# A two-layer decoder trunk on one core: opening with matmuls on constants, sums of squares on VectorE, two loads in halves, small tiles padded

## The chip, the cores and the metric

The kernel runs on one core of one Trainium2 chip. The time is device microseconds (us) from the start to the end of one execution, the median of several runs. The five engines that matter are TensorE (PE in the profile, its weight loads PEld), VectorE (DVE), ScalarE (ACT), GpSimd (POOL) and the queue SP, which here issues most of the DMAs.

## What is computed

The reference is a trunk of two residual layers over 256 tokens of width 2048, all in float32. The pieces that matter here are the norm and the input projection of the first layer:

```python
h = x
hn = rmsnorm(h, norm_w[0])            # x * rsqrt(mean(x*x) + eps) * w
proj = hn @ w_in                      # 2048 -> 12320 columns
z_a, xbc, dt_raw, z_b, u, v = split(proj)
xbc = silu(causal_depthwise_conv(xbc, conv_w, conv_b))   # x, B and C of the scan
dt = softplus(dt_raw + dt_bias)
```

Then come a chunked state-space scan over 32 heads in 8 groups, a gated spatial mixing of 16 groups, an output projection, a second layer of differential attention with 16 heads, its output projection, and a last RMSNorm.

## The kernel before

**Layout.** Activations are kept transposed, channels on the partitions: `xw` holds the normed input as 16 blocks (k = 0 to 15) of 128 channels by 256 tokens. Float32 precision is kept by splitting each operand in a high half, rounded to the matmul's reduced float32 (`fp32r`), and a low half, which is the rest. For activations `put_split` (L202) does this: ScalarE writes the high half (L204), VectorE the low one (L205). For weights `split` (L115) does it: ScalarE writes `wh` (L118), VectorE `wl` (L119), on 1024 elements a partition at a time.

**Projections.** Weights come in tiles of 128 x 2048 (1 MB) in the order in which they are used; `fetch` (L122) loads one with one DMA on SP, `halves` (L127) splits it in two halves. `t_half` (L132) takes one half: a run of eight matmuls of 512 columns, `wh` against high and low activations together (L136), and a run of eight of 256 columns, `wl` against the high activations (L140). A block of 128 output channels is two halves, thus 16 matmuls of either kind. `tok_proj` (L159) computes 512 channels for all tokens with three products a step (L170 to L172). There are three buffers each for the raw weights, `wh` and `wl`.

**Order.** The tile framework orders the instructions of every engine ahead of time: each engine takes, of what its estimate says is ready, the instruction that stands first in the program text. The chip then runs each engine's instructions strictly in that order. `issue_after` sets what it encloses behind a given instruction on the engine of that instruction.

**The opening (L209 to L262).** SP loads x in pieces (the first in two halves), the small weight `wdt` of the dt projection, and the first two weight tiles (`raw_first`, those of B and C) in halves, all interleaved: x first half, `wdt`, x second half, then by turns half a weight tile and the next four blocks of x. `wd` is `wdt` split into high and low columns (L240, L241). The loop at L243 splits each block of x into `xw` and multiplies it for dt (L245). Then B and C are multiplied by halves (`t_half`, L136 and L140). The norm's factor isn't in `xw`; it is applied behind the projections. It is made at L253 to L262: ScalarE squares x behind the last split of the opening (L256), POOL adds the sixteen blocks up (L257 to L261), and `token_rstd` (L181) sums over the partitions with a matmul against `ones` (L187), takes the power -1/2 on POOL (L191) and spreads the result over the partitions with a matmul against `ident` (L194), to `rb` (L199).

**What follows.** Blocks x0_0 and x0_1 are the next two projections (`conv_block`, L326), then B1, C1, x1_0, x1_1 and the gate z. The dt stage (L265 to L317) makes dt from `pdt` with `rt0`: an exponential, then a series in some 17 small POOL operations (L290 to L302), two transposes on TensorE (L305), a cumulative sum (L309), and its way to all partitions through DRAM.

**Constants.** At L90 to L104: `col` (per-channel constants) by ScalarE's DMA queue, then on POOL `ident`, `ones`, `mhalf`, `maskT` and two small loads. `ms` (L177, L184) is a tile of two numbers a partition, two buffers of it, in a pool that also holds larger temporary tiles; the pools allocated behind that one hold `xw`, `ya` and everything after.

```python
def t_half(ps, hv, x, half, first, last):
    wh, wl = hv
    for i in range(8):                                       # L134 to L137
        k = half * 8 + i
        pe.matmul(ps, lhsT=wh[:, i, :], rhs=x[:, k, :, :].rearrange("p a b -> p (a b)"), start=first and k == 0, stop=False)
    for i in range(8):                                       # L138 to L141
        k = half * 8 + i
        pe.matmul(ps[:, 256:512], lhsT=wl[:, i, :], rhs=x[:, k, 0, :], start=False, stop=last and k == 15)
```

Of the kernel before, what the change touches and what calls it, by code (L numbers as in the profile page):

```python
# [9 lines left out]
F32 = mybir.dt.float32  # L10
F32R = mybir.dt.float32r
AF = mybir.ActivationFunctionType
ALU = mybir.AluOpType
# [4 lines left out]
P = 128  # L18
# [54 lines left out]
def hybrid_trunk(ctx: ExitStack, tc: tile.TileContext, xT, cols, dskip, dtp, lnw, lnb, sgub, wsT,  # L73
                 wdt, w0, wo0, w1, wo1, outT):
    nc = tc.nc
    v, act, pe, pool = nc.vector, nc.scalar, nc.tensor, nc.gpsimd

    const = ctx.enter_context(tc.tile_pool(name="const", bufs=1))
    wp = ctx.enter_context(tc.tile_pool(name="wp", bufs=3))
    ev = ctx.enter_context(tc.tile_pool(name="ev", bufs=2))  # L80
# [5 lines left out]
    def aux(name):  # L86
        return aux_p.tile([P, 512], F32, tag="aux", name=name)


    col = const.tile([P, N_COLS], F32, name="col")  # L90
    act.dma_start(col, cols)
    ident = const.tile([P, P], F32, name="ident")
    make_identity(nc, ident)
    ones = const.tile([P, P], F32, name="ones")
    pool.memset(ones, 1.0)
    mhalf = const.tile([P, 2], F32, name="mhalf")
    pool.memset(mhalf, -0.5)
    maskT = const.tile([P, P], F32, name="maskT")
# [10 lines left out]
    def c1(i):  # L109
        return col[:, i:i + 1]  # L110


    last_split = [None, None]

    def split(raw, shape, nm):  # L115
        wh = wp.tile([P] + shape, F32R, tag="wh", name=f"wh_{nm}")
        wl = wp.tile([P] + shape, F32R, tag="wl", name=f"wl_{nm}")
        last_split[0] = act.activation(wh, raw, AF.Copy).ins  # L118
        last_split[1] = v.tensor_tensor(wl, raw, wh.bitcast(F32), op=ALU.subtract).ins  # L119
        return wh, wl  # L120

    def fetch(src, nm):  # L122
        raw = wp.tile([P, 2048], F32, tag="raw", name=f"raw_{nm}")
        nc.sync.dma_start(raw, src)
        return raw

    def halves(src, inner, nm):  # L127
        raw = fetch(src, nm).rearrange("p (a b) -> p a b", b=inner)
        n = 2048 // inner // 2
        return [split(raw[:, h * n:(h + 1) * n, :], [n, inner], f"{nm}_{h}") for h in range(2)]  # L130

# [11 lines left out]
    def t_accum(ps, src, x, first, last, nm):  # L143

        hv = halves(src, P, nm)
        for half in range(2):
            t_half(ps, hv[half], x, half, first, last)

    def acc(nm):
        return acc_p.tile([P, 512], F32, tag="acc", name=f"acc_{nm}")  # L150
# [8 lines left out]
    def tok_proj(srcs, x, nm):  # L159
        ps = [acc(f"{nm}_{i}") for i in range(2)]  # L160
        for kq in range(4):
            hv = halves(srcs[kq], 512, f"{nm}_{kq}")
            for kk in range(4):
                k = kq * 4 + kk
                wh, wl = hv[kk // 2]
                wh, wl = wh[:, kk % 2, :], wl[:, kk % 2, :]
                for tb in range(2):
                    xh = x[:, k, 0, tb * P:(tb + 1) * P]
                    xl = x[:, k, 1, tb * P:(tb + 1) * P]
                    pe.matmul(ps[tb], lhsT=xh, rhs=wh, start=k == 0, stop=False)  # L170
                    pe.matmul(ps[tb], lhsT=xh, rhs=wl, start=False, stop=False)  # L171
                    pe.matmul(ps[tb], lhsT=xl, rhs=wh, start=False, stop=k == 15)  # L172
        return ps

    def pow_mhalf(dst, ssum, n, scale, nm):

        ms = ev.tile([P, 2], F32, tag="ms", name=f"ms_{nm}")  # L177
        v.tensor_scalar(ms[:, :n], ssum, scale, EPS, op0=ALU.mult, op1=ALU.add)
        pool.tensor_tensor(dst, ms[:, :n], mhalf[:, :n], op=ALU.pow)

    def token_rstd(sqs, nm, copy=True):  # L181

        pcs = [aux(f"pc{tb}_{nm}") for tb in range(2)]
        ms = ev.tile([P, 2], F32, tag="ms", name=f"ms_{nm}")  # L184
        for tb in range(2):
            for i, sq in enumerate(sqs):
                pe.matmul(pcs[tb][:, 0:1], lhsT=sq[:, tb * P:(tb + 1) * P], rhs=ones[:, 0:1],  # L187
                          start=i == 0, stop=i == len(sqs) - 1)
            v.tensor_scalar(ms[:, tb:tb + 1], pcs[tb][:, 0:1], 1.0 / D, EPS, op0=ALU.mult, op1=ALU.add)
        rt = const.tile([P, 2], F32, tag="rt", name=f"rt_{nm}", bufs=2)  # L190
        pool.tensor_tensor(rt, ms, mhalf, op=ALU.pow)  # L191
        pb = aux(f"pb_{nm}")
        for tb in range(2):
            pe.matmul(pb[:, tb * P:(tb + 1) * P], lhsT=rt[:, tb:tb + 1].broadcast_to([P, P]),  # L194
                      rhs=ident, start=True, stop=True)
        if not copy:
            return rt, pb[:, 0:S]
        rb = const.tile([P, S], F32, tag="rb", name=f"rb_{nm}", bufs=1)
        act.activation(rb, pb[:, 0:S], AF.Copy)  # L199
        return rt, rb  # L200

    def put_split(dst, src, scale):  # L202

        act.activation(dst[:, 0, :], src, AF.Copy, scale=scale)  # L204
        v.scalar_tensor_tensor(dst[:, 1, :], src, scale, dst[:, 0, :].bitcast(F32),  # L205
                               op0=ALU.mult, op1=ALU.subtract)


    with ExitStack() as l0:  # L209
        s1 = l0.enter_context(tc.tile_pool(name="ssd1", bufs=1))  # L210

        sqs = s1.tile([P, S], F32, name="sqs")
# [8 lines left out]
        def split_first(i, half):  # L221
            raw = first[i][0][:, half * 1024:(half + 1) * 1024].rearrange("p (a b) -> p a b", b=P)
            first[i][1][half] = split(raw, [8, P], f"first{i}_{half}")

        with tc.tile_pool(name="start", bufs=4) as st:
            wdt_raw = st.tile([P, KB, 32], F32, name="wdt_raw", bufs=1)
# [10 lines left out]
                first_half(i % 2, i // 2)  # L237
            wd = st.tile([P, KB, P], F32R, name="wd", bufs=1)
            pool.memset(wd[:, :, 64:128].bitcast(F32), 0.0)
            act.activation(wd[:, :, 0:32], wdt_raw, AF.Copy)  # L240
            v.tensor_tensor(wd[:, :, 32:64], wdt_raw, wd[:, :, 0:32].bitcast(F32), op=ALU.subtract)  # L241
            pdt = acc("dt")
            for k in range(KB):  # L243
                put_split(xw[:, k], xr[k // 4][:, k % 4, :], c1(C_NW0 + k))
                pe.matmul(pdt, lhsT=wd[:, k, :], rhs=xw[:, k].rearrange("p a b -> p (a b)"),  # L245
                          start=k == 0, stop=k == KB - 1)
                if k % 4 == 3:
                    split_first(k // 4 % 2, k // 8)
# [4 lines left out]
            sq = st.tile([P, 4, 4, S], F32, name="sq", bufs=1)  # L253
            with tc.issue_after(last_split[0]):
                for i in range(4):
                    act.activation(sq[:, i], xr[i], AF.Square)  # L256
            pool.tensor_tensor(sq[:, 0], sq[:, 0], sq[:, 1], op=ALU.add)  # L257
            pool.tensor_tensor(sq[:, 2], sq[:, 2], sq[:, 3], op=ALU.add)
            pool.tensor_tensor(sq[:, 0], sq[:, 0], sq[:, 2], op=ALU.add)
            pool.tensor_tensor(sq[:, 0, 0:2], sq[:, 0, 0:2], sq[:, 0, 2:4], op=ALU.add)  # L260
            pool.tensor_tensor(sqs, sq[:, 0, 0, :], sq[:, 0, 1, :], op=ALU.add)  # L261
            rt0, rb0 = token_rstd([sqs], "n0")  # L262


# [152 lines left out]
        def ssd_finish(g, y, sz):  # L417
            n = f"g{g}"
            v.tensor_tensor(y, y, sz[:, :, (g % 2) * S:(g % 2 + 1) * S], op=ALU.mult)
            ss = sp.tile([P, 2], F32, tag="ss", name=f"ss_{n}")  # L420
            for c in range(2):
                junk = sp.tile([P, S], F32, tag="junk", name=f"junk_{n}_{c}")
                act.activation(junk, y[:, c, :], AF.Square, accum_out=ss[:, c:c + 1])
            rg = sp.tile([P, 2], F32, tag="rg", name=f"rg_{n}")
            pow_mhalf(rg, ss, 2, 1.0 / S, n)
            for c in range(2):
                act.activation(y[:, c, :], y[:, c, :], AF.Copy, scale=rg[:, c:c + 1])
            ps4 = aux(f"ps4_{n}")
            for b in range(2):
                for c in range(2):  # L430
                    pe.transpose(ps4[:, b * S + c * P:b * S + (c + 1) * P], y[:, c, b * P:(b + 1) * P], ident)
            for b in range(2):
                put_split(ya[:, 2 * g + b], ps4[:, b * S:(b + 1) * S], c1(C_SNW + 2 * g + b))
# [13 lines left out]
    with ExitStack() as l0b:  # L447
# [13 lines left out]
        for tb in range(2):  # L461
            junk = gp_.tile([P, D], F32, tag="junk", name=f"vjunk{tb}", bufs=1)
            act.activation(junk, vt[:, tb, :], AF.Square, bias=nmu[:, tb:tb + 1], accum_out=vq[:, tb:tb + 1])
        vr = g1.tile([P, 2], F32, name="vr")
        pow_mhalf(vr, vq, 2, 1.0 / D, "ln")
        ws_t = sb_t = None
        for j in range(16):
            n = f"j{j}"
# [33 lines left out]
            for c in range(2):  # L502
                pe.matmul(pm[:, c * P:(c + 1) * P], lhsT=vt[:, c, j * P:(j + 1) * P], rhs=ws_t[:, j % 4, :],
                          start=True, stop=True)
# [46 lines left out]
    act.dma_start(res, xT)  # L551
    sqp = out_proj(wo0, "o0", lambda n: put_split(xw[:, n], res[:, n, :], c1(C_NW1 + n)))
    rt1, rb1 = token_rstd(sqp, "n1")


# [127 lines left out]
    n = 0  # L683
# [70 lines left out]
```

## Time and profile before

| | |
|---|---|
| median of 3 runs | 1724.22 us (1722.86 to 1724.52) |
| the profiled execution: its time | 1724.63 us |
| the profiled execution: its span | 1722.9 us |
| TensorE matmuls: busy, share, count | 1702.2 us, 99%, 9232 |
| TensorE weight loads: busy, share | 1460.7 us, 85% |
| VectorE: busy, share, instructions | 1126.6 us, 65%, 1704 |
| ScalarE: busy, share, instructions | 990.1 us, 57%, 1521 |
| POOL: busy, share, instructions | 106.0 us, 6%, 159 |
| moved by DMA | 318.68 MB, mean 185 GB/s |

The profile is one execution recorded by the chip. The span goes from its first instruction to its last; the execution's own time is 1.7 us longer. Busy shares are averages over the whole span. Matmuls are pipelined, so that the durations of neighbours overlap; the distance between starts tells their rate. In the rows, "a<-b" names what is written and what is read, "[0.70 <-ACT wh_first]" is idle time of that engine just before the instruction and what ended it, "x8" merges eight instructions.

### The profile page before, as it was taken

The page shows a single profiled execution, that of the slowest core. Times are in us where ns is not written, and L with a number is a line of the kernel's source. Part 1 is how long each engine was busy: PE and PEld are TensorE (multiplying, and loading weights), DVE is VectorE, ACT ScalarE, POOL GpSimd, SP SyncE. Part 2 cuts the span into 40 slices and gives each one's busy share as a digit, 9 for nine tenths or more (in the row PEclk, how much of TensorE's full clock was granted, in tenths as well). Part 3 has the DMA queues.
Part 4 walks back from the last instruction along what each step waited for, and adds up shares of the span by engine and source line. Part 5 has one row for each costly group of instructions (what it writes and reads, how often), then busy time and mean ns, then how long its engine had stood idle before and what let it go on. Part 6 is the DMA issues. An engine that isn't in the chain of part 4 may idle for free.

```text
span 1722.9 us, 23833 instructions
## 1 busy us (share of the span) xinstructions
PE 1702.2 (99%) x9232; PEld 1460.7 (85%) x9232; DVE 1126.6 (65%) x1704; ACT 990.1 (57%) x1521; POOL 106.0 (6%) x159
## 2 busy tenths in 40 slices
PE   7999999999999999999999999999999999999997
PEld 6888888888888888888888888888888888888886
DVE  6897869545777665556566666757576666655554
ACT  6776776546777744445455555555554555555443
POOL 3200000100000011110000000000000000001110
PEclk9999999999999999999999999999999999999998
DMA  7555444655655565555455455455545555445552
GB/s 254 207 175 195 172 159 171 218 198 191 216 205 173 194 236 184 193 194 172 172 188 177 171 173 191 173 173 173 184 169 184 174 180 184 171 172 196 195 191 104
DMA packets 46290, 318.68 MB, mean 185 GB/s; under 512 B 5280, under 2 KB 5584, under 8 KB 9440
## 3 DMA queue, kind: packets, MB, share of 16 engines
q1 hardware_dynamic: 44400, 310.30, 51.3%
q0 software_dynamic: 1344, 4.24, 0.9%
q10 hardware_dynamic: 432, 2.61, 0.4%
q8 instruction: 72, 1.18, 0.3%
q14 instruction: 42, 0.34, 0.1%
HBM read 315.00 MB, written 2.13 MB: 184 GB/s over the span
## 4 chain that ended last, share of the span: by engine, by line
PE 95%; DVE 1%; ACT 1%; issue 1%; POOL 1%; DMA 0%; SPq 0%; DVEq 0%; POOLq 0%; ACTq 0%
PE acc_o L136 13%; PE acc_q L136 7%; PE acc_k L136 7%; PE acc_o L140 7%; PE acc_v L170 5%; PE acc_v L172 5%; PE acc_v L171 5%; PE acc_q L140 3%; PE acc_g L172 3%; PE acc_k L140 3%; PE acc_g L170 3%; PE acc_g L171 3%; PE acc_u L136 3%; PE acc_zb L136 3%; PE acc_x L136 3%; PE acc_u L140 2%
## 5 line engine op out<-in xcount | busy, mean ns | idle before, releaser
L118 ACT ACTIVATE wh_v<-raw_v 128x1024 fp32r<-128x1024 f32 x96 | 101.8, 1060 | 109.1 <-PE acc_v L172 88.7
L119 DVE TENSOR_TENSOR wl_v<-raw_v,wh_v 128x1024 fp32r<-128x1024 f32 x96 | 117.6, 1225 | 68.3 <-ACT wh_v L118 67.4
L171 PE MATMUL acc_v<-wl_v,xw 128*128 128x512 f32 x384 | 152.2, 396 | 0.0
L172 PE MATMUL acc_v<-wh_v,xw 128*128 128x512 f32 x384 | 151.6, 395 | 0.0
L170 PE MATMUL acc_v<-wh_v,xw 128*128 128x512 f32 x384 | 142.8, 397 | 0.0
L136 PE MATMUL acc_q<-xw,wh_q 128*128 128x512 f32 x512 | 131.8, 393 | 0.0
L119 DVE TENSOR_TENSOR wl_g<-raw_g,wh_g 128x1024 fp32r<-128x1024 f32 x64 | 78.4, 1226 | 80.6 <-ACT wh_g L118 80.6
L136 PE MATMUL acc_k<-xw,wh_k 128*128 128x512 f32 x512 | 130.8, 395 | 0.0
L118 ACT ACTIVATE wh_g<-raw_g 128x1024 fp32r<-128x1024 f32 x64 | 67.9, 1060 | 80.5 <-PE acc_g L172 53.5
L119 DVE TENSOR_TENSOR wl_q<-raw_q,wh_q 128x1024 fp32r<-128x1024 f32 x64 | 77.8, 1225 | 52.0 <-ACT wh_q L118 46.5
L118 ACT ACTIVATE wh_k<-raw_k 128x1024 fp32r<-128x1024 f32 x64 | 67.8, 1059 | 70.2 <-PE acc_q L136 30.2
L118 ACT ACTIVATE wh_q<-raw_q 128x1024 fp32r<-128x1024 f32 x64 | 67.8, 1059 | 68.3 <-PE acc_g L172 23.9
L136 PEld LDWEIGHTS acc_k<-xw,wh_k 128*128 128x128 f32 x512 | 91.6, 188 | 16.2
L136 PEld LDWEIGHTS acc_q<-xw,wh_q 128*128 128x128 f32 x512 | 90.5, 188 | 15.6
L172 PE MATMUL acc_g<-wh_g,xw 128*128 128x512 f32 x256 | 101.5, 397 | 0.0
L171 PE MATMUL acc_g<-wl_g,xw 128*128 128x512 f32 x256 | 101.0, 394 | 0.0
L119 DVE TENSOR_TENSOR wl_k<-raw_k,wh_k 128x1024 fp32r<-128x1024 f32 x64 | 78.3, 1224 | 26.8 <-ACT wh_k L118 26.7
L170 PE MATMUL acc_g<-wh_g,xw 128*128 128x512 f32 x256 | 92.2, 396 | 0.0
L170 PEld LDWEIGHTS acc_v<-wh_v,xw 128*128 128x128 f32 x384 | 72.0, 187 | 16.5
L172 PEld LDWEIGHTS acc_v<-wh_v,xw 128*128 128x128 f32 x384 | 72.0, 188 | 16.3
L171 PEld LDWEIGHTS acc_v<-wl_v,xw 128*128 128x128 f32 x384 | 72.0, 188 | 16.0
L140 PE MATMUL acc_q<-xw,wl_q 128*128 128x256 f32 x512 | 73.8, 281 | 0.0
(500 smaller groups left out, 4012.6 us busy)
## 6 DMA issues: line engine op xcount, KB each, us to landing
raw_v<-in_w_dram SPq DMA_DIRECT2D x48, 1024.0 KB, 4.8
raw_q<-in_w_dram SPq DMA_DIRECT2D x32, 1024.0 KB, 4.7
raw_k<-in_w_dram SPq DMA_DIRECT2D x32, 1024.0 KB, 4.8
raw_g<-in_w_dram SPq DMA_DIRECT2D x32, 1024.0 KB, 4.8
raw_x<-in_w_dram SPq DMA_DIRECT2D x16, 1024.0 KB, 4.8
raw_z<-in_w_dram SPq DMA_DIRECT2D x16, 1024.0 KB, 4.8
raw_u<-in_w_dram SPq DMA_DIRECT2D x16, 1024.0 KB, 4.8
raw_zb<-in_w_dram SPq DMA_DIRECT2D x16, 1024.0 KB, 4.8
```

The lines of the kernel that those rows point to most:

```text
L118: last_split[0] = act.activation(wh, raw, AF.Copy).ins
L119: last_split[1] = v.tensor_tensor(wl, raw, wh.bitcast(F32), op=ALU.subtract).ins
L136: pe.matmul(ps, lhsT=wh[:, i, :], rhs=x[:, k, :, :].rearrange("p a b -> p (a b)"), start=first and k == 0, stop=False)
L140: pe.matmul(ps[:, 256:512], lhsT=wl[:, i, :], rhs=x[:, k, 0, :], start=False, stop=last and k == 15)
L170: pe.matmul(ps[tb], lhsT=xh, rhs=wh, start=k == 0, stop=False)
L171: pe.matmul(ps[tb], lhsT=xh, rhs=wl, start=False, stop=False)
L172: pe.matmul(ps[tb], lhsT=xl, rhs=wh, start=False, stop=k == 15)
```

## The change

The change has four parts.

- **Constants and matmuls on them.** `ones` is now made ahead of `ident`. ScalarE copies a piece of it into a new tile `warm`, and TensorE multiplies `ones` by itself 14 times, in float32, 128 columns each, into a PSUM tile that nobody reads.
- **Loads.** `fetch` takes a number of parts; the tiles of x0_0 and x0_1 are loaded in two halves each, all others whole as before. The loads of the opening keep their order.
- **Opening.** The split of `wd` moves in the text from ahead of the loop over k to behind the first `put_split`. The five additions of the squares move from POOL to VectorE, set behind the last `wl` of the opening there.
- **Padding.** `ms` grows from 2 to 16 numbers a partition; `warm` has 32. With that the 14 matmuls take a buffer of the `aux` pool once.

```diff
--- before.py
+++ after.py
@@ -89,10 +89,16 @@
 
     col = const.tile([P, N_COLS], F32, name="col")
     act.dma_start(col, cols)
+    ones = const.tile([P, P], F32, name="ones")
+    pool.memset(ones, 1.0)
     ident = const.tile([P, P], F32, name="ident")
     make_identity(nc, ident)
-    ones = const.tile([P, P], F32, name="ones")
-    pool.memset(ones, 1.0)
+
+    warm = const.tile([P, 32], F32, name="warm")
+    act.activation(warm, ones[:, 0:32], AF.Copy)
+    pw = aux("warm")
+    for i in range(14):
+        pe.matmul(pw[:, 0:P], lhsT=ones, rhs=ones, start=True, stop=True)
     mhalf = const.tile([P, 2], F32, name="mhalf")
     pool.memset(mhalf, -0.5)
     maskT = const.tile([P, P], F32, name="maskT")
@@ -119,13 +125,15 @@
         last_split[1] = v.tensor_tensor(wl, raw, wh.bitcast(F32), op=ALU.subtract).ins
         return wh, wl
 
-    def fetch(src, nm):
+    def fetch(src, nm, parts):
         raw = wp.tile([P, 2048], F32, tag="raw", name=f"raw_{nm}")
-        nc.sync.dma_start(raw, src)
+        n = 2048 // parts
+        for i in range(parts):
+            nc.sync.dma_start(raw[:, i * n:(i + 1) * n], src[:, i * n:(i + 1) * n])
         return raw
 
     def halves(src, inner, nm):
-        raw = fetch(src, nm).rearrange("p (a b) -> p a b", b=inner)
+        raw = fetch(src, nm, 2 if nm in ("x0_0", "x0_1") else 1).rearrange("p (a b) -> p a b", b=inner)
         n = 2048 // inner // 2
         return [split(raw[:, h * n:(h + 1) * n, :], [n, inner], f"{nm}_{h}") for h in range(2)]
 
@@ -174,21 +182,21 @@
 
     def pow_mhalf(dst, ssum, n, scale, nm):
 
-        ms = ev.tile([P, 2], F32, tag="ms", name=f"ms_{nm}")
+        ms = ev.tile([P, 16], F32, tag="ms", name=f"ms_{nm}")
         v.tensor_scalar(ms[:, :n], ssum, scale, EPS, op0=ALU.mult, op1=ALU.add)
         pool.tensor_tensor(dst, ms[:, :n], mhalf[:, :n], op=ALU.pow)
 
     def token_rstd(sqs, nm, copy=True):
 
         pcs = [aux(f"pc{tb}_{nm}") for tb in range(2)]
-        ms = ev.tile([P, 2], F32, tag="ms", name=f"ms_{nm}")
+        ms = ev.tile([P, 16], F32, tag="ms", name=f"ms_{nm}")
         for tb in range(2):
             for i, sq in enumerate(sqs):
                 pe.matmul(pcs[tb][:, 0:1], lhsT=sq[:, tb * P:(tb + 1) * P], rhs=ones[:, 0:1],
                           start=i == 0, stop=i == len(sqs) - 1)
             v.tensor_scalar(ms[:, tb:tb + 1], pcs[tb][:, 0:1], 1.0 / D, EPS, op0=ALU.mult, op1=ALU.add)
         rt = const.tile([P, 2], F32, tag="rt", name=f"rt_{nm}", bufs=2)
-        pool.tensor_tensor(rt, ms, mhalf, op=ALU.pow)
+        pool.tensor_tensor(rt, ms[:, 0:2], mhalf, op=ALU.pow)
         pb = aux(f"pb_{nm}")
         for tb in range(2):
             pe.matmul(pb[:, tb * P:(tb + 1) * P], lhsT=rt[:, tb:tb + 1].broadcast_to([P, P]),
@@ -237,11 +245,12 @@
                 first_half(i % 2, i // 2)
             wd = st.tile([P, KB, P], F32R, name="wd", bufs=1)
             pool.memset(wd[:, :, 64:128].bitcast(F32), 0.0)
-            act.activation(wd[:, :, 0:32], wdt_raw, AF.Copy)
-            v.tensor_tensor(wd[:, :, 32:64], wdt_raw, wd[:, :, 0:32].bitcast(F32), op=ALU.subtract)
             pdt = acc("dt")
             for k in range(KB):
                 put_split(xw[:, k], xr[k // 4][:, k % 4, :], c1(C_NW0 + k))
+                if k == 0:
+                    act.activation(wd[:, :, 0:32], wdt_raw, AF.Copy)
+                    v.tensor_tensor(wd[:, :, 32:64], wdt_raw, wd[:, :, 0:32].bitcast(F32), op=ALU.subtract)
                 pe.matmul(pdt, lhsT=wd[:, k, :], rhs=xw[:, k].rearrange("p a b -> p (a b)"),
                           start=k == 0, stop=k == KB - 1)
                 if k % 4 == 3:
@@ -254,11 +263,12 @@
             with tc.issue_after(last_split[0]):
                 for i in range(4):
                     act.activation(sq[:, i], xr[i], AF.Square)
-            pool.tensor_tensor(sq[:, 0], sq[:, 0], sq[:, 1], op=ALU.add)
-            pool.tensor_tensor(sq[:, 2], sq[:, 2], sq[:, 3], op=ALU.add)
-            pool.tensor_tensor(sq[:, 0], sq[:, 0], sq[:, 2], op=ALU.add)
-            pool.tensor_tensor(sq[:, 0, 0:2], sq[:, 0, 0:2], sq[:, 0, 2:4], op=ALU.add)
-            pool.tensor_tensor(sqs, sq[:, 0, 0, :], sq[:, 0, 1, :], op=ALU.add)
+            with tc.issue_after(last_split[1]):
+                v.tensor_tensor(sq[:, 0], sq[:, 0], sq[:, 1], op=ALU.add)
+                v.tensor_tensor(sq[:, 2], sq[:, 2], sq[:, 3], op=ALU.add)
+                v.tensor_tensor(sq[:, 0], sq[:, 0], sq[:, 2], op=ALU.add)
+                v.tensor_tensor(sq[:, 0, 0:2], sq[:, 0, 0:2], sq[:, 0, 2:4], op=ALU.add)
+                v.tensor_tensor(sqs, sq[:, 0, 0, :], sq[:, 0, 1, :], op=ALU.add)
             rt0, rb0 = token_rstd([sqs], "n0")
 
 
```

## Rows read from the trace of the kernel before

**Rows 1.** The page, part 1: busy time, share of the span, instructions.

```profile
PE 1702.2 (99%) x9232; PEld 1460.7 (85%) x9232; DVE 1126.6 (65%) x1704; ACT 990.1 (57%) x1521; POOL 106.0 (6%) x159
```

**Rows 2.** Waits of TensorE, whole kernel: us in total, times, longest.

```profile
PE acc_dt L245 <- DVE wd L241: 8.0, 1, 8.0
PE pda L305 <- POOL xp_x L334: 1.3, 1, 1.3
```

**Rows 3.** The chain of waits in order of time: start us, us, what.

```profile
13.29 0.43 PE acc_B L136
...
17.54 1.84 PE acc_C L136 x8
...
24.03 0.91 PE acc_B L140 x8
...
27.71 1.83 PE acc_x L136 x8
```

**Rows 4.** Windows: us, busy of PE, PEld, DVE, ACT, POOL, granted clock, DMA share, GB/s.

```profile
12.00:16.00 4.00, 4.00 (x10) 2.92 (x10) 3.67 (x9) 4.00 (x9) 0.00 (x0) 1.00 1.04 426
...
60.00:64.00 4.00, 2.87 (x17) 2.19 (x15) 4.00 (x7) 2.43 (x5) 3.56 (x6) 1.00 0.53 160
```

**Rows 5.** Timeline, POOL; then the chain at L194, four records.

```profile
0.81 0.20 POOL masks.py:197 MEMSET ident<- 128x128 f32 x1 [0.29 <-POOLq L745]
...
41.74 0.44 PE pb_n L194 x4
```

**Rows 6.** Timeline of the opening: start us, us, engine, line, operation.

```profile
4.42 1.28 ACT L204 ACT_TABLE_LOAD   x1 [4.42 <-DMA xr<-in_xT_dram]
...
6.53 0.61 ACT L240 ACTIVATE wd<-wdt_raw 128x512 fp32r<-128x512 f32 x1
...
9.65 1.06 ACT L118 ACTIVATE wh_first<-raw_first 128x1024 fp32r<-128x1024 f32 x1 [1.71 <-DMA raw_first<-in_w_dram]
...
10.76 2.08 PE L136 MATMUL acc_B<-xw,wh_first 128*128 128x512 f32 x4 [0.70 <-ACT wh_first L118]
11.28 1.71 ACT L204 ACTIVATE xw<-xr,col 128x256 fp32r<-128x256 f32 x4 [0.46 <-DMA xr<-in_xT_dram]
...
12.63 0.66 PE L245 MATMUL acc_dt<-xw,wd 128*128 128x512 f32 x1
...
17.83 1.66 DVE L205 SCALAR_TENSOR_TENSOR xw<-xr,col,xw 128x256 fp32r<-128x256 f32 x4
...
18.95 3.88 ACT L256 ACTIVATE sq<-xr 128x1024 f32<-128x1024 f32 x4
...
22.74 1.04 ACT L118 ACTIVATE wh_x<-raw_x 128x1024 fp32r<-128x1024 f32 x1
```

**Rows 7.** Timeline, POOL sums and VectorE beside; VectorE by shape.

```profile
21.02 2.42 POOL L257 TENSOR_TENSOR sq<-sq 128x1024 f32<-128x1024 f32 x1 [16.02 <-ACT sq L256]
...
23.81 3.07 DVE L119 TENSOR_TENSOR wl_x<-raw_x,wh_x 128x1024 fp32r<-128x1024 f32 x1 [3.18 <-PE acc_dt L245]
...
26.80 2.62 DVE L269 TENSOR_TENSOR dt_zT<-dt_lo 32x256 f32<-32x256 f32 x1
...
31.81 1.61 POOL L261 TENSOR_TENSOR sqs<-sq 128x256 f32<-128x256 f32 x1
...
L119 DVE TENSOR_TENSOR wl_v<-raw_v,wh_v 128x1024 fp32r<-128x1024 f32 x96 | 117.6, 1225 | 68.3 <-ACT wh_v L118 67.4 <-PE acc_k L140 0.9
```

**Rows 8.** Timeline, POOL chain of dt, TensorE behind it; then the chain.

```profile
51.38 0.32 POOL L290 TENSOR_TENSOR dt_w<-dt_e,dt_w 128x64 f32<-128x64 f32 x1 [1.92 <-DVE dt_w L289]
...
64.19 0.39 PE L305 MATMUL pda<-ident,dt_z 128*32 128x128 f32 x2 [1.32 <-POOL xp_x L334]
...
64.59 0.23 PE acc_z L170
```

**Rows 9.** The first two loads of raw_x on SP: durations, starts, time to landing.

```profile
L124 SPq DMA_DIRECT2D raw_x<-in_w_dram x2: 327/507/687, 7.8 to 17.9; - x2
...
DMA to landing us min/median/max: 4.7/8.4/12.2
```

## The prediction

> **What bounds the kernel now.** I began with the page: TensorE is busy for 99% of the span [rows 1], so a change pays only where it removes something TensorE waits for or runs slowly through. Next came TensorE's waits over the whole kernel [rows 2]: 8.0 us before the first matmul and 1.3 us in the transposes of the dt stage (L305); a third, 0.7 us for the first split weights, is read from the timeline [rows 6]. Two more of a microsecond or less stand in the last row norm, which the change leaves alone. Then the chain of waits, read as a clock [rows 3]: one line there is one matmul or a run of them, and its length is what it adds to the chain. At 13.29 us a matmul of 512 columns adds 0.43 us; from 17.54 us eight add 1.84 us, 0.23 each. 512 columns in 0.43 us are the 1.2 GHz level, in 0.23 us the 2.4 GHz level with some overhead. The granted clock does not show this: it reads 1.00 in 12 to 16 us, where the matmuls are slow [rows 4], so I read the level from the spacing. It rose at some point between these two rows, after TensorE had run without a gap from 10.76 us [rows 6].
>
> How much is lost? Ahead of block x0, which begins at 27.71 us [rows 3], TensorE has 48 matmuls of 512 columns (16 for dt, 16 each for B and C) and 32 of 256. At 1.83 and 0.91 us per eight [rows 3] that is 11.0 + 3.6 = 14.6 us. So 13.1 us go to waiting and to the slow clock. Behind x0 only the 1.3 us at L305 are left to win.
>
> **Warm-up matmuls.** `ones` takes `ident`'s place in POOL's queue, so it is ready near 0.81 + 0.20 = 1.0 us [rows 5]; `ident` and what follows it on POOL, two small DMA issues among them, come 0.2 us later, and none of the longer waits is for them [rows 2]. The two fp32 products of L194 appear as four records and 0.44 us on the chain [rows 5], 0.22 us each at full rate; at half rate 0.44, so 14 of them last at most 6.2 us, from 1.1 to 7.3 us. In front of the first xw ScalarE now has a table load of 1.28 us that starts only when x arrives [rows 6]. The copy of `ones` draws it to about 1.1 us, so everything behind it can start up to 1.28 us sooner: dt's first matmul could go at 8.0 - 1.28 = 6.7 us. ScalarE already runs the first xw ahead of the copy of wd at 6.53 [rows 6], so moving that copy behind k = 0 in the text moves little. The warm-ups thus end last, at 7.3, and dt's first four run until 8.2 at full rate. TensorE will then have run from 1.1 us without a gap; I take the clock as risen.
>
> **What the data allows.** The first weights end ScalarE's wait for their DMA at 9.65, so matmul B starts at 10.76 as before [rows 6]: the loads keep their order, and the DMA engines are full (share 1.04 at 12 to 16 us [rows 4]). Four matmuls of B (k 0 to 3) end at 11.7. k = 4 needs the next piece of x, which ends ScalarE's next wait for a DMA at 11.28, and dt's matmul for it starts at 12.63 [rows 6]; I leave it there. From then I let TensorE run through what is left: 12 of dt and 12 of B at 0.229 (5.5 us), 16 low ones of B (1.8) and all of C (5.5), 12.8 us, so x0 begins at 25.4. Nothing gates that: the last low halves of x end at 17.83 + 1.66 = 19.5, before the turn of k = 12 (near 20); ScalarE has split all of B's and C's weights when it starts the squares at 18.95, and x0's first weights end at 22.74 + 1.04 = 23.8 [rows 6]. 27.71 becomes 25.4: **2.3 us won**. Bounds: most 3.9 us, where ScalarE's 23.8 is the limit and low matmuls of B fill the gaps; least, nothing, if the clock is not up at 10.76.
>
> The gap from 8.2 to 10.76 is the weak point. The longest wait that full-rate matmuls follow is 1.32 us, and 0.23 us spacing stands right behind it [rows 8]; 2.6 us is not shown. I let the clock hold, since 2.6 is nearer to that row than to the 8 us before the first matmul. The Trainium skill, "TensorE: Matmul & The Clock Gate", section "Why this matters for your kernels", warns of idle gaps between bursts of matmuls, after which the clock is back at half. By that the 2.3 us could be lost whole; it is the first rival below.
>
> **Sums of squares on VectorE.** Off POOL go five additions, from 21.02 to 31.81 + 1.61 = 33.4 us [rows 7]. VectorE needs 1.22 us for two inputs of 1024 elements [rows 7]; by elements the five are 1.22 x (3 + 0.5 + 0.25) = 4.6 us. Back it gets what POOL's sums seem to cost it: beside them the split at 23.81 took 3.07 instead of 1.22 us, and the sum of 256 elements at 26.80 took 2.62 us where a quarter of 1.22 is 0.3 [rows 7]; together 4.1 us. So VectorE is about even. But its queue is in order: the second sum waits for the fourth square (18.95 + 3.88 = 22.8 [rows 6]), and if four sums and the three dt sums (0.3 to 0.4 each) stand ahead of x0's low half, that half ends at 22.8 + 3.4 + 1.1 + 1.2 = 28.5, where TensorE wants it at 25.4 + 1.8 = 27.2: 1.3 us lost. If it stands between them, nothing. I take 0.4, nearer to nothing, because x0's high half is ready at 23.8, amid the sums.
>
> The row norm is ready some 7 us sooner (22.8 + 3.4 = 26.2 against 33.4), and with it the way to L305: the column sums, the power, the broadcast, and POOL's chain from 51.38 until it lets L305 go at 64.19 [rows 8]. Matmuls are issued in a fixed order, so a chain that ends sooner saves only the 1.32 us waited there, and TensorE itself comes 2.3 us sooner. Bounds: 1.3 us won; 2.3 us lost, if the chain did not move at all. I take 0.4 won.
>
> **Moves at no cost.** x0_0 and x0_1 are loaded in two halves: SP issues two more DMAs in a stretch where it waits for buffers. x0_0 is issued at 7.8, and the slower of the first two loads lands 12.2 us after its issue [rows 9], thus at 20.0 at the latest; ScalarE takes it up at 22.74, behind the squares, which are the cover. Without it a half would land perhaps a microsecond sooner. The `warm` tile, 128 bytes, and `ms`, whose two buffers grow by 56 bytes each, move what is allocated behind them, xw and ya too. No row gives an address. I take nothing; for the ends I use the step between the 1.83 and 1.84 us of eight matmuls [rows 3], 0.5% or 9 us either way.
>
> **Sum:** -2.3 + 0.4 - 0.4 = -2.3 us, from the profiled execution's 1724.63 (span 1722.9 and 1.7 around it) to 1722.3. That execution is 0.4 us above the median, 1724.22; against the median I forecast 1721.9, 0.13% faster. A measurement of this kernel can tell about 0.2%, 3.4 us, from no change, so the likeliest finding is "same".
>
> **Rivals.** (1) The clock is low again at 10.76, or never rose. Then dt, B and C run as now, x0 begins near 27.7, and L305 and VectorE's loss cancel: 1724.2, give or take 1. For it: the unshown 2.6 us of idling. Against: six to seven busy microseconds ahead of it, and the clock held over 1.32. Chance 0.17.
> (2) The order comes out well: low matmuls fill the gaps (0.8 us more), x0's low half stands among the sums, L305 no longer waits: 2.3 + 0.8 + 1.3 = 4.4 us, at the bound 3.9 + 1.3 = 5.2: 1719.0 to 1719.8. For it: the norm's inputs come 7 us sooner. Against: in the present order dt's and B's matmuls of k 4 stand ahead of B's low ones. Chance 0.25.
> (3) Slower: VectorE's in-order queue becomes the late engine. VectorE is full from 60 to 64 us [rows 4], with the convolutions; if these move up among the splits of x0 and x1, a split waits behind them and TensorE stalls at its low matmuls. It decides once the stalls pass the 2.3 won; to be slower by over 3.4 us they must sum to 5.7, five splits late by one operation of 1.22 each: 1728. Against: TensorE crosses that stretch now without a wait for VectorE [rows 2]. Chance 0.06.
> (4) The addresses matter after all, in all 9232 matmuls: 9 us either way. Chance 0.06, half for each sign.
>
> **How the numbers follow.** The forecast keeps 0.46, and its 1721.9 is the predicted time. The range, 1718.8 to 1725.2, takes in rival 2 at its low end and rival 1 with its microsecond at the high end, and leaves out (3) and (4). Faster by over 0.2% (below 1720.8): all of (2), 0.25, a fifth of the forecast for the spread of its terms, 0.09, and 0.03 of (4): 0.37. Slower: 0.06 of (3), 0.03 of (4), 0.01 of (1): 0.1. Within: 0.53.
>
> **What would show it.** Right: the table load before 3 us; matmuls of `ones` from about 1.1 us; dt's first at 7 to 7.5 and no 0.43 us spacing behind 10.76; x0 near 25.4; the sums on VectorE at 1.22 us each beside x0's splits; L305's wait between 0 and 2 us; runs of eight still at 1.83 us. Wrong: 0.43 us spacing behind 10.76 (rival 1), TensorE idle in front of wl_x (rival 3), another time for eight matmuls in mid-kernel (rival 4).

## The result, and the profile after

The changed kernel takes **1736.23 us**, the median of 4 runs (1734.94 to 1737.25); the kernel before took 1723.54 beside it (1722.11 to 1724.52). The ratio is 1.0075, with a 95% interval of 1.0063 to 1.0088: slower by about 13 us. The profiled execution took 1736.36 us, its span is 1734.6.

The page of the changed kernel, part 1, answers to [rows 1]:

```profile
PE 1719.4 (99%) x9260; PEld 1473.4 (85%) x9260; DVE 1126.7 (65%) x1709; ACT 989.0 (57%) x1520; POOL 91.9 (5%) x154
```

TensorE is busy for 17.2 us more, with only 28 records more, the warm-ups, which last 4.8 us. It does not wait more: the list of its waits has 6.4 us in all, and the two of [rows 2] are now 1.3 us and none.

```profile
PE acc_B L144 <- ACT wh_first L124: 1.8, 1, 1.8
PE acc_dt L254 <- DVE wd L253: 1.3, 1, 1.3
```

So its matmuls have become longer. The chain of waits of the changed kernel shows where, in the middle of the output projection, far from the opening (start, length, what):

```profile
649.83 1.87 PE acc_o L144 x8
651.70 0.95 PE acc_o L148 x8
652.65 1.86 PE acc_o L144 x8
654.51 0.94 PE acc_o L148 x8
```

The same place in the chain of the kernel before:

```profile
654.32 0.94 PE acc_o L140 x8
655.27 1.83 PE acc_o L136 x8
657.10 0.91 PE acc_o L140 x8
```

Eight of 512 columns take 1.86 to 1.87 us, where the kernel before takes 1.83, and eight of 256 take 0.94 to 0.95, where it takes 0.91 and 0.94 by turns. This is so in every stage with feature matmuls. For finer numbers I worked out, from the records behind 30 us, the mean distance between the starts of neighbouring matmuls of one kind, the **pace** (distances over 300 ns left out). Feature matmuls, those with the weights stationary, on xw went from 229.6 to 232.6 ns (512 columns) and from 118.6 to 120.3 (256); those of the output projections from 228.8 to 233.0 and from 115.6 to 118.6 (the 96 of the last block's own form, L531, counted in); the token matmuls, with the data stationary, from 233.3 to 232.4. There are 128 feature tiles on xw and 62 of the output projections, of 16 matmuls of either width each, and 2304 token matmuls: 2048 x (3.0 + 1.7) + 992 x (4.2 + 3.0) - 2304 x 0.9 ns = **14.7 us**. That is the whole loss and a little more; the opening gave the rest back.

The opening, timeline of TensorE (start, length, operation, the wait in brackets), then two pieces of the chain, then two windows (columns as in [rows 4]):

```profile
1.06 4.82 PE L101 MATMUL warm<-ones 128*128 128x128 f32 x28 [1.06 <-POOL ones L93]
7.16 0.70 PE L254 MATMUL acc_dt<-xw,wd 128*128 128x512 f32 x2 [1.28 <-DVE wd L253]
8.09 0.90 PE L254 MATMUL acc_dt<-xw,wd 128*128 128x512 f32 x2 [0.23 <-DVE xw L213]
10.81 2.01 PE L144 MATMUL acc_B<-xw,wh_first 128*128 128x512 f32 x4 [1.83 <-ACT wh_first L124]
```

```profile
13.35 0.43 PE acc_B L144
...
14.77 0.23 PE acc_B L144
...
26.70 1.86 PE acc_x L144 x8
```

```profile
8.00:12.00 4.00, 2.08 (x5) 1.38 (x6) 1.64 (x4) 2.23 (x5) 0.00 (x0) 0.86 0.97 366
12.00:16.00 4.00, 4.00 (x16) 3.05 (x16) 4.00 (x11) 4.00 (x8) 0.00 (x0) 0.71 1.03 422
```

The warm-ups and dt's early start are there, but behind the wait of 1.83 us the granted clock fell (0.86, then 0.71), and matmuls of 0.43 us, the 1.2 GHz level, stand until past 14 us. Block x0 begins at 26.70, not 27.71 [rows 3] and not 25.4.

### The profile page after: what moved, and what is told of

Its sections match the earlier page's. It is cut to its first block, busy times and chain, and to the rows that moved or that the text cites. A ratio compares the mean times of both kernels' runs of the same rounds, so it can differ in the third digit from the quotient of the medians.

```text
span 1734.6 us, 23891 instructions
## 1 busy us (share of the span) xinstructions
PE 1719.4 (99%) x9260; PEld 1473.4 (85%) x9260; DVE 1126.7 (65%) x1709; ACT 989.0 (57%) x1520; POOL 91.9 (5%) x154
## 4 chain that ended last, share of the span: by engine, by line
PE 97%; ACT 1%; issue 1%; DVE 1%; DMA 0%; SPq 0%; DVEq 0%; POOLq 0%; POOL 0%; ACTq 0%
PE acc_o L144 13%; PE acc_k L144 7%; PE acc_q L144 7%; PE acc_o L148 7%; PE acc_v L178 5%; PE acc_v L180 5%; PE acc_v L179 5%; PE acc_q L148 4%; PE acc_k L148 4%; PE acc_zb L144 3%; PE acc_u L144 3%; PE acc_x L144 3%; PE acc_g L179 3%; PE acc_g L178 3%; PE acc_g L180 3%; PE acc_u L148 2%
## 5 line engine op out<-in xcount | busy, mean ns | idle before, releaser
L148 PEld LDWEIGHTS acc_q<-xw,wl_q 128*128 128x128 f32 x512 | 70.3, 188 | 5.1
```

## The experiments

The edits tried change either the opening or where tiles lie. In the storage plans of the built kernels the split weights (wh, wl) and their data (xw, ya, yb) begin at these bytes within 256; **distance** is data less weights for feature matmuls (weights stationary), weights less data for token matmuls (data stationary), each within 256. Paces as above, in ns:

| kernel | weights | data | feature, token distance | on xw 512 / 256 | output 512 / 256 | token | us | ratio to before (95%) |
|---|---|---|---|---|---|---|---|---|
| before | 0 | 64 | 64, 192 | 229.6 / 118.6 | 228.8 / 115.6 | 233.3 | 1723.54 | 1 |
| after | 128 | 0 | 128, 128 | 232.6 / 120.3 | 233.0 / 118.6 | 232.4 | 1736.23 | 1.0075 (1.0063 to 1.0088) |
| e1 | 128 | 192 | 64, 192 | 229.5 / 118.3 | 228.8 / 115.6 | 233.3 | 1722.27 | 0.9989 (0.9980 to 0.9998) |
| e2 | 0 | 128 | 128, 128 | 232.6 / 120.4 | 232.9 / 118.6 | 232.5 | 1737.17 | 1.0082 (1.0066 to 1.0097) |
| e3 | 192 | 64 | 128, 128 | 232.5 / 120.3 | 232.9 / 118.6 | 232.5 | 1735.92 | 1.0073 (1.0059 to 1.0087) |
| e4 | 192 | 0 | 64, 192 | 229.5 / 118.2 | 228.8 / 115.6 | 233.3 | 1720.71 | 0.9984 (0.9975 to 0.9993) |
| v1 | 128 | 128 | 0, 0 | 230.6 / 120.5 | 230.5 / 119.0 | 227.5 | 1719.67 | 0.9976 (0.9967 to 0.9985) |
| v2 | 0, token 64 | 64 | 64, 0 | 229.4 / 118.1 | 228.7 / 115.5 | 227.5 | 1707.52 | 0.9909 (0.9893 to 0.9926) |

The first expectations still speak of places within 128 bytes; the map below showed that 256 is the measure.

**The padding undone, and alone.** e1 is the changed kernel with the old `ms`; e2 is the kernel before with the new one, and nothing else of the change.

```
e1, both ms tiles:  -tile([P, 16], F32, tag="ms")  +tile([P, 2], F32, tag="ms")
e2, both ms tiles:  -tile([P, 2], F32, tag="ms")   +tile([P, 16], F32, tag="ms")
```

> The changed kernel with ms back at 2 numbers, so that xw, ya and yb lie 64 bytes lower, at 64 instead of 0 modulo 128; every engine's order is that of the changed kernel. Theory (addresses set TensorE's pace): eight matmuls of 512 columns go back from 1.87 to 1.83 us, and the time is that of the changed kernel less some 14 us, near 1721 to 1722. Rival (the pace comes from the new order or from the warm-ups): eight stay at 1.87 us and the time near 1736.

> The kernel before with ms of 16 numbers and nothing else: xw, ya and yb move from 64 to 0 modulo 128, every engine's order is that of the kernel before. Theory (addresses): eight matmuls of 512 columns take 1.86 to 1.87 us, time near 1737. Rival (order or warm-ups): 1.83 us, time near 1724.

Measured: e1 takes 1722.27 us, e2 1737.17. Two small tiles that no matmul reads carry the loss both ways: 1736.23 - 1722.27 = 14.0 us out (14.8 by the ratios, each to the kernel before beside it), 1737.17 - 1723.32 (before, beside it) = 13.9 us in. Every engine has the same instructions in the same order as in the kernel each was made from. In e1's chain the eights are those of before again:

```profile
650.69 1.83 PE acc_o L144 x8
652.53 0.91 PE acc_o L148 x8
```

**Which place counts?** Both operands moved by a longer `warm`, of which 32 columns are used as ever (e3), and only the weights (e4).

```
-    warm = const.tile([P, 32], F32, name="warm")
+    warm = const.tile([P, 48], F32, name="warm")
e4 also:  tile([P, 2], F32, tag="ms")
```

> The changed kernel with warm of 48 numbers instead of 32: raw, wh and wl move from 0 to 64 modulo 128, and xw, ya, yb from 0 to 64. Theory a (only the place of the moving operand counts, 64 being fast): projections with xw as the moving operand run at 1.83 us per eight, near 1722. Theory b (the places of both operands count, and only stationary at 0 with moving at 64 is fast): 1.86 us per eight or more, near 1736.

> The changed kernel with warm of 48 and ms of 2 numbers: raw, wh and wl at 64 modulo 128, xw, ya, yb at 0. Both theories: eight of the projections with xw moving stay at 1.86 us or more. The products with xw stationary and wh, wl moving (three lines of the token projections, 0.233 us each now) have their moving operand at 64 here: theory a and b both expect them at about 0.229, some 8 us less than the changed kernel in all, near 1728; if pace has nothing to do with which operand moves, they stay at 0.233 and the time near 1736.

Measured: e3 is as slow as the changed kernel, 1735.92 us; e4 is fast, 1720.71. For e3 theory b's number came, and a's did not; e4 came out as neither had it. In e4 the data lie where they lie in the slow changed kernel, and the weights where they lie in the slow e3, so no place of one operand is bad by itself. Left is the place of one operand relative to the other. I first took this for two 64-byte halves of 128 bytes, and measured it by itself.

**The map.** m1 moves one operand in steps of 32 bytes, in groups u of 16 (w, v, u: feature form with the weights at three places; t: token form); m2 is the grid of all 8 by 8 places, feature form. m1, m2 and the m3 further down ran once each.

```
for so in range(8):
    for mo in range(8):
        wide(8 * so, 8 * mo, f"s{so}m{mo}")   # 16 matmuls of 512 columns, then 16 of 256
```

> No part of the model is computed: x is copied to the output, and TensorE runs groups of products in the kernel's two forms, with nothing else to do on the chip. Groups w: 16 products of 512 and 16 of 256 columns with the stationary operand at 0 and the moving one at 0, 32, 64, ... 992 bytes modulo 2048; groups v: stationary at 64; groups u: stationary at 16, moving at 0, 16, 32, 48; groups t: the token projections' form, stationary at 0, moving at 0 to 480. Theory (only the distance of the two addresses modulo 128 counts, by which half of a 128-byte line each falls in): w at 0 takes 0.2325 us a product and at 64 about 0.2295, repeated every 128 bytes; v the same by distance; t between 0.2325 and 0.2335. Rival (the distance is not what counts, but traffic of the other engines on certain addresses): all groups w alike.

> Computes no part of the model: x is copied to the output, and behind that every pair of places is timed, s for the stationary and m for the moving operand, 0 to 7 steps of 32 bytes each (s2m5: weights 64 bytes into their tile, data 160 bytes into theirs; both tiles begin at the same place of a 256-byte ring), sixteen matmuls of 512 columns and sixteen of 256 in each group. In the map before, the pace came back after every eight steps: distance 0 took 226.7 to 227.6 ns per 512 columns, distance 64 bytes 228.8, all other distances 232.8 to 234.0; per 256 columns the best was distance 32 with 116.7, distance 64 117.8, distance 0 119.5. Theory D (only the distance, moving less stationary, taken within 256 bytes counts): each diagonal of the grid has one pace within 1 ns: 227 (0), 229 (2), 233 to 234 (the rest) per 512 columns, 116.7 (1) per 256 columns. Theory E (the places themselves count too): the diagonals differ; the 114.1 ns per 256 columns of the one earlier group with s2m0, against 117.8 at the same distance with the weights at place 0, speaks for it, and then the best pair for 256 columns is 114 or below.

In m1 the pace of 512 columns comes back after every eight steps, four times over: 226.7 to 227.6 ns at distance 0, 228.8 at 64 bytes, 232.8 to 234.0 at the other six; the token form has 227, 229 and 233 to 234 at the same distances. So the ring is 256 bytes, and the theory of halves falls. In m2 each diagonal agrees within 1.2 ns for 512 columns and 1.4 for 256, bar one of the 128 groups, s4m2 with 256 columns (114.1, its diagonal else 117.7 to 117.8). The 114.1 of m1 stood at s2m0; there the grid has 117.8, so it goes with no place; both have distance 192, and what makes a run of 256 columns so fast now and then stays open. For starts at multiples of 32 bytes, where the kernels above have all these tiles, theory D holds. Off that grid it does not: in m1's groups u, with the weights 16 bytes into their tile, 512 columns take 233.4, 232.7, 228.2 and 232.2 ns at distances -16, 0, 16 and 32, so distance 0 is slow there. The second and third of them in m1's chain:

```profile
233.22 3.72 PE uAB L51 x16
...
238.83 3.65 PE uAC L51 x16
```

The second row of m2's grid, the weights one step into their tile, the data 0 to 7 steps, in the chain (some of the 256 ones left out):

```profile
71.31 3.73 PE s1m L48 x16
...
76.93 3.64 PE s1m L48 x16
80.57 1.91 PE s1m L52 x16
82.48 3.73 PE s1m L48 x16
86.22 1.87 PE s1m L52 x16
88.08 3.66 PE s1m L48 x16
91.75 1.88 PE s1m L52 x16
93.63 3.74 PE s1m L48 x16
...
99.28 3.72 PE s1m L48 x16
...
104.90 3.74 PE s1m L48 x16
...
110.54 3.73 PE s1m L48 x16
```

The second group (distance 0) takes 3.64 us, the fourth (64 bytes) 3.66, all others 3.72 to 3.74. For 256 columns 32 bytes is best (1.87), and distance 0 is among the slow (1.91).

**Everything at distance 0.** The kernel before had its feature matmuls at the second best distance, but its token matmuls at a slow one. v1 gives both distance 0.

```
both ms tiles:  -tile([P, 16], F32, tag="ms")  +tile([P, 32], F32, tag="ms")
```

> The changed kernel with ms of 32 columns in place of 16, nothing else: the split weights and the normed input then begin at the same place of a 256-byte ring (distance 0), in the kernel before at distance 64 (feature matmuls) and 192 (token matmuls), in the changed kernel at 128. Theory D: the 2304 token matmuls go from 233.3 to 227.7 ns (-13 us against the kernel before), the 512-column feature matmuls from 229.6 to 227.6 (-5 us over 2700), the 256-column ones from 118.6 and 115.6 to 119.5 to 120 (+6 us over 2700): together -12 us, 1709 to 1714 us, ratio 0.991 to 0.995. Rival, the earlier theory of 64-byte halves (same half is slow whatever the distance): as slow as the changed kernel, 1735 to 1737 us, ratio 1.007 to 1.009.

Measured: 1719.67 us. The halves are refuted, but theory D had 1709 to 1714. The token matmuls do what the map says, 227.5 ns. The 512-column feature matmuls do not: 230.6 where the map has 227.6. In the model eights of 512 and of 256 alternate; the map has sixteen alike. m3 has the alternation by itself, for all pairs of distances.

```
for j in range(4):
    ...   # 8 matmuls of 512 columns, weights at place h, then 8 of 256, weights at place l
```

> Computes no part of the model: x is copied to the output, and behind that eights of 512 and eights of 256 columns alternate as in the feature matmuls, four of each in a group, for every pair of distances (0 to 7 steps of 32 bytes) of the weights of the 512 and of those of the 256. Open: at distance 0 the 512-column feature matmuls of the model took 230.6 ns, in the grid, where sixteen of a kind follow one another, 227.6. Theory F (the change of size costs: the first five or so matmuls behind it run at another pace): a group at distances 0, 0 takes 4 x (8 x 230.6 + 8 x 120) = 11.22 us and one at 2, 2 takes 4 x (8 x 229 + 8 x 116.5) = 11.06 us, as in the model. Rival G (other engines' accesses cost it in the model, which this run does not have): 0, 0 takes 4 x (8 x 227.6 + 8 x 119.5) = 11.11 us and 2, 2 takes 4 x (8 x 228.9 + 8 x 117.8) = 11.10 us, the same.

> Feature matmuls at distance 64 bytes as in the kernel before, token matmuls at distance 0: ms of two columns, the split tiles 64 columns longer, and the token matmuls' weights 64 bytes into them; mask, skip and step constants move into the first stage's storage to make room. Every engine's instructions are those of the changed kernel in the same order. Theory D with the paces of the model's own traces: 2304 token matmuls at 227.5 in place of 233.3 ns give 13.4 us, the feature matmuls stay at 229.5 and 118.3: 1707 to 1711 us, ratio 0.990 to 0.993. Rival: token matmuls gain, but something else becomes the bound as TensorE speeds up (loads, evictions): 1712 to 1720.

m3's chain, two alternations each at distances 0 and 0, at 64 and 64, at 128 and 128 bytes:

```profile
26.49 1.84 PE h7l_p L48 x8
28.33 0.95 PE h7l_p L51 x8
29.28 1.84 PE h7l_p L48 x8
31.12 0.95 PE h7l_p L51 x8
...
227.82 1.83 PE h5l_p L48 x8
229.64 0.94 PE h5l_p L51 x8
230.59 1.83 PE h5l_p L48 x8
232.42 0.91 PE h5l_p L51 x8
...
429.33 1.86 PE h3l_p L48 x8
431.19 0.95 PE h3l_p L51 x8
432.14 1.87 PE h3l_p L48 x8
434.01 0.95 PE h3l_p L51 x8
```

These are the runs of eight of v1, of the kernel before and of the changed kernel, with no other engine at work; at 64 and 64 bytes the eights of 256 take 0.94 and 0.91 us by turns here too. By the starts a group of four alternations takes 11.17 us at 0, 0 and 11.03 at 64, 64 (F: 11.22 and 11.06; G: 11.11 and 11.10): **theory F**. At distance 0 the five matmuls behind a change of width take 228 to 236 ns, the next three 226 to 227; both m3 and v1 show it. Of the 64 pairs only 64 with 192 bytes (2.750 us for 8 + 8) beats 64 with 64 (2.757); 0, 0 takes 2.792 and 128, 128 takes 2.811.

v2 takes the best of each: features at 64 bytes as before, token matmuls at 0. To make room, three constants move to a pool of the first stage.

```
-        wh = wp.tile([P] + shape, F32R, tag="wh", name=f"wh_{nm}")
-        wl = wp.tile([P] + shape, F32R, tag="wl", name=f"wl_{nm}")
+        off = 16 if shape[1] == 512 else 0
+        wh, wl = [wp.tile([P, 1088], F32R, tag=g, name=f"{g}_{nm}")[:, off:off + 1024]
+                  .rearrange("p (a b) -> p a b", b=shape[1]) for g in ("wh", "wl")]
...
both ms tiles:  -tile([P, 16], F32, tag="ms")  +tile([P, 2], F32, tag="ms")
```

Measured: **1707.52 us** (1707.31 to 1707.57), as theory D had it, 15 us under the kernel before and 29 under the changed one, with the changed kernel's instructions in the same order. Its page, then one window in the token projections (us, busy, matmuls, granted clock, DMA share, GB/s), of the changed kernel first and then of v2:

```profile
PE 1690.3 (99%) x9260; PEld 1462.3 (86%) x9260; DVE 1126.5 (66%) x1709; ACT 987.7 (58%) x1520; POOL 93.1 (5%) x154
```

```profile
340.00:400.00 60.00, 60.00 (x260) 1.00 0.58 204
```

```profile
340.00:400.00 60.00, 60.00 (x267) 1.00 0.56 196
```

Seven matmuls more in 60 us, at the same granted clock. 2304 x (233.3 - 227.5) ns = 13.4 us of the gain over e1, 14.8 us, are the token matmuls.

**The opening, with the places of before.** Each is e1 with one edit: 36 warm-ups (o1), none (o2), the sums back on POOL (o3).

```
o1:  -    for i in range(14):   +    for i in range(36):
o2:  -    pw = aux("warm")  and the loop of 14 matmuls
o3:  -    with tc.issue_after(last_split[1]):  and  v.tensor_tensor(sq[:, 0], ...)  and four more
     +    pool.tensor_tensor(sq[:, 0], ...)  and four more
```

> The changed kernel with small ms (fast addresses) and 36 instead of 14 warm-up products, which last until about 10.6 us. Theory (the idle time ahead of 10.8 us let the clock fall, and x0 starts late for that): no spacing of 0.43 us behind 10.8, x0 begins near 25.4 us, about 1.0 us sooner than with 14, time near 1721. Rival (the gates of the loads decide, not the clock): x0 near 26.5, no gain.

> The changed kernel with small ms and without its 14 products; the rest of the change stays. Theory (the warm-ups brought the clock up 2.7 us sooner on the second rise): x0 begins near 27.5 us, time about 1 us more than with the warm-ups, near 1723. Rival (they bought nothing, the clock fell anyway): x0 near 26.5 and no difference.

> The changed kernel with small ms and the five sums of squares back on POOL. Theory (the wait at the dt transposes went away with the sums on VectorE): the wait of about 1.3 us there is back, time about 1.3 us more, near 1723.5. Rival (it went because the order around it was written anew): no such wait, no difference.

Measured: 1721.96 us, ratio 0.9993 (0.9984 to 1.0002); 1722.58, 0.9994 (0.9985 to 1.0003); 1721.82, 0.9990 (0.9981 to 0.9999). All three overlap with e1, so no part of the opening can be told from nothing by its time. In the profiles x0 begins at 24.72 in e1's (1719.38 us, among the fastest of e1's eleven runs, 1719.09 to 1723.44), at 27.84, 26.47 and 26.71 in theirs. The clock held in o1's, as its theory had it, but x0 came no sooner; o2's 26.47 is its rival's figure; o3's wait at the dt transposes is 0.3 us, nearer to its rival than to 1.3. One profile of each doesn't part the edits from when the loads land. In o1's it is the next piece of x that is late: ScalarE waits for it until 12.56, where it had it at 10.94 in the changed kernel's.

## Why the prediction was wrong

**The step that failed is "Moves at no cost"**, its last sentences: "No row gives an address. I take nothing". The term taken as 0 measured 14.0 us (after against e1) and 14.7 by the paces: the `ms` tiles move the data by 64 bytes, 32 for each buffer (the prediction had 56 each), which takes the distance from 64 to 128 bytes (e1 against after). Rival 4 named the mechanism, that the addresses matter in all matmuls, but with a chance of 0.06, and its "9 us either way" was too small: the bound came from 1.83 and 1.84 us, two runs of eight in one placement, and such rows hold nothing of another placement. An edit that moves the operands of nearly all matmuls needed a rival of its own weight. That the time would change in mid-kernel, "another time for eight matmuls", was the sign named for it, and it is what the chain shows.

**The rest of the change** is e1 against before: a ratio of 0.9989, 1.9 us won (0.3 to 3.4). The sum of -2.3 lies inside, but that is partly luck, for its terms did not come: in the changed kernel's profile x0 won 1.0 us where the sum has 2.3, VectorE lost nothing where it has 0.4, and L305 won 1.3 where it has 0.4. Step by step:

- Warm-ups and table load: right. The load stands at 1.25 us, matmuls of `ones` at 1.06 to 5.88 (at most 7.3 was forecast), dt's first at 7.16 (7 to 7.5), though not behind the warm-ups but behind a wait of 1.28 us for `wd`.
- "I let the clock hold": wrong in the changed kernel's profile. The gap was 1.83 us and not 2.6, and the clock fell all the same, rival 1's mechanism, so x0 won 1.0 us of the 2.3. In e1's the first weights were there sooner, TensorE waited 0.40 us for them, and x0 began at 24.72. By the spacing of the matmuls behind the gaps the clock held in the profiles of e1, e3 and o1 and fell in those of e4, v1, v2 and o3. The Trainium skill, "TensorE: Matmul & The Clock Gate", section "Why this matters for your kernels", warns that an idle gap between bursts brings the clock back to half. The trace agrees in kind: 1.8 us without a matmul, then a granted clock of 0.71. But this gap is shorter than those that the Trainium skill warns of there; by this trace a shorter one can do it.
- Sums on VectorE: the 0.4 lost did not come. TensorE has no wait for a low half of x0, since the queue put that split between the sums, as VectorE's timeline of the changed kernel shows:

```profile
22.52 1.23 DVE L268 TENSOR_TENSOR sq<-sq 128x1024 f32<-128x1024 f32 x1 [0.67 <-ACT sq L265]
23.66 1.22 DVE L125 TENSOR_TENSOR wl_x<-raw_x,wh_x 128x1024 fp32r<-128x1024 f32 x1
24.80 1.22 DVE L269 TENSOR_TENSOR sq<-sq 128x1024 f32<-128x1024 f32 x1
...
31.27 0.40 DVE L271 TENSOR_TENSOR sqs<-sq 128x256 f32<-128x256 f32 x1
```

- "Some 7 us sooner" for the norm was wrong: the last sum ends at 31.67 against 33.42 [rows 7], 1.75 us, because splits and dt's sums took turns with the five.
- L305: no wait is left, so 1.3 us and not 0.4. It isn't shown to be the change's doing: e2, in the order of before, has no wait there either, o3, with the sums on POOL, 0.3, and o1 and o2, with the sums on VectorE, 0.5 and 0.8.
- Rival 3, VectorE late: not seen. Rival 2 came out at L305 and in x0's low half, which stands among the sums; x0 itself came later than it had it.

What of the mechanism stays open: why the distance of the two operands sets the pace. The runs show that it does, not which reads meet.

## What to carry to other kernels

When a bound engine becomes uniformly slower or faster, compare runs of the same instruction in mid-kernel before looking at the edited stage. A tile's size is also the address of everything behind it: undo the sizes alone, and the edit alone. Where TensorE sets the end, try placing its two operands against each other on a 256-byte ring (here 64 bytes for alternating widths, 0 for uniform 512 columns, with both starts at multiples of 32 bytes).

## What the runs showed of the hardware that was not expected

- The pace of these matmuls depends on the distance of the two operands' starts within 256 bytes: 226.7 to 227.7 ns at 0, 228.8 to 230.0 at 64, 232.3 to 234.3 elsewhere for 512 columns, up to 3% apart (m2). With both starts at multiples of 32 bytes the places themselves make no difference beyond that; with both 16 bytes off, distance 0 takes 232.7 (m1). The Trainium skill, "SBUF — State Buffer", section "SBUF: two separate sides", says that on the engines' side only the port pair shared by VectorE and GpSimd brings contention, and that TensorE never waits on another engine. That is not contradicted: the map shows the effect with the other engines idle. The Trainium skill, "SBUF — State Buffer", section "Operand start alignment", asks only for a multiple of the element size, and says that its runs timed nothing; here the timing differs among legal starts.
- After a change of width the pace at distance 0 takes about five matmuls to settle (228 to 236 ns, then 226 to 227; m3 and v1), so a map of one width alone misjudged v1 by some 8 us.
- The length of a gap alone does not say whether the clock falls. In o1, behind 36 warm-ups without a gap, it held over 1.74 us; in o3, behind sparse matmuls, it fell in 1.54 us. That what ran ahead of the gap decides is not shown. TensorE's timeline and chain of o1, then of o3:

```profile
13.64 0.50 PE L254 MATMUL acc_dt<-xw,wd 128*128 128x512 f32 x1 [1.74 <-DVE xw L213]
```

```profile
14.62 0.69 PE acc_B L144 x3
```

```profile
12.05 0.80 PE L254 MATMUL acc_dt<-xw,wd 128*128 128x512 f32 x1 [1.54 <-DVE xw L213]
```

```profile
12.84 0.43 PE acc_B L144
13.27 0.43 PE acc_dt L254
```
